# A Hymba block on one Trainium2 core: GLU's weights in plain blocks, 52 products ahead of u, and v's shifted rows on GpSimd's queue

## The chip, the core and the metric

One core of a Trainium2 chip runs the whole block as one program. The metric is the device time of one execution in microseconds (us), and kernels are compared by the median of their runs. A profile is of one execution.

## The reference

One layer: RMSNorm, one combined projection, a state space model (SSM) with a gated linear unit (GLU) beside stick-breaking attention, a shared output projection, and a gate from a per-layer embedding. 2048 tokens, 1024 channels, 8 heads of 64.

```python
h = x
hn = rmsnorm(h, mix_norm_g)
u, g_ssm, q, k, v, g_attn = split(hn @ w_in)            # 512 columns each
y_ssm = glu(gelu(s5(u)), w_glu, b_glu) * silu(g_ssm)      # val * sigmoid(gate) of z @ w_glu + b_glu
# attention in blocks of 128 queries, strictly causal
z = q @ k.T / 8
log_stay = where(strict, log_sigmoid(-z), 0)
later = cumsum(log_stay, reverse) - log_stay
weights = where(strict, exp(log_sigmoid(z) + later), 0)
y_att = (weights @ v) * silu(g_attn)
h = h + concat(y_ssm, y_att) @ w_out
h = h + sigmoid(rmsnorm(h) @ w_ple_gate) * (p @ w_ple_proj)
```

In stick-breaking attention the weight of a key is the difference of two neighbouring running products of 1 − sigmoid(z). So the kernel may multiply the running products by differences of neighbouring rows of v, and this is why it needs v beside v shifted by one row.

## The kernel before

**Tiles and number format.** The 2048 tokens are 16 tiles of 128 (NT), the 1024 channels 8 blocks of 128 (NC8). A float32 matrix is split into a high and a low part of type fp32r, and a product is three (high × high, high × low, low × high): `mm3` (L539, its three products are L544, L545, L546), `mm3x` (L714), and the three steps in `attn_proj` (L757) and `attn_block` (L824). A weight is loaded by `load_w`: DMA on SyncE's queue into a stage `wst` (L489), high part `w_w` on ScalarE (L494) and low part on VectorE (L79), or, where it has no scale, `split` (L516 and L68).

**Stages.** `phase_u` (0 to 142 us of the profile) makes u in 8 turns T of 256 tokens: 4 blocks of columns (ct) × 8 blocks of channels × 3 products. For T = 0 the loop over channel blocks is outside, so that a weight block is used as it arrives; ahead of its first product stand HOT = 18 products of a zero tile `idle` (L634) into the same bank, which the first real product overwrites. The norm of T = 2 and later is a chain: ScalarE squares and sums x (L601), VectorE and GpSimd make `rs_x` (L75, L510), ScalarE scales x (L603), TensorE turns it (`ps_x`, L529). Beside it VectorE computes the SSM's tables (`ssm_chain`). Then come the SSM with the gates and the first projections of attention (142 to 305), attention (305 to 1090), and the output projection with the embedding's gate (from 1090).

**Attention.** Four pairs of heads (hp 0 to 3) follow each other 8 steps apart in one loop over steps. In a step, `attn_block` works on one query tile of each active pair, and `attn_proj` makes q, k, v and the gate of the tile two steps ahead. The GLU, its weights (`glu_load`, two halves of four blocks `wst`, L489) and sums of weights run in the last ten steps and just before.

`attn_proj` leaves q, k, gate and v of a tile in `qn`. Then v − shifted v is formed on GpSimd:

```python
    nc.sync.dma_start(vb[1:], vr[:P - 1])
    if i + 1 < NT:
        nc.sync.dma_start(A.v[i + 1][:1].rearrange("p h d -> p (h d)"), vr[P - 1:])
    nc.gpsimd.tensor_tensor(vb, vr, vb, op=ALU.subtract)
```

The first transfer (L765) moves 127 rows of v down by one partition, the second (L767) the last row into the first row of the next tile; L768 subtracts when both have landed. Behind it on GpSimd stand the power for the norm of q and k (`rs_qk`, L510) and in `attn_block` the strict mask: `affine_select` (L831) on `px`, which ScalarE wrote (L828) and VectorE's scan (L833) reads. The scan releases the banks of `ps_z`; its result is turned (`ps_wt`, L529), made into `ws` (L847) and multiplied by v (`ps_o`, L855).

**Order.** The program's text doesn't set the order. `_ORDER` is a compressed table that lists, engine by engine, which of the remaining instructions comes next; `arrange` (L1387) turns neighbours in it into dependencies. The five engines are TensorE (PE), VectorE (DVE), ScalarE (ACT), GpSimd (POOL) and SyncE (SP), whose list holds nearly all DMA issues. Each engine works its list in order, so a waiting instruction holds what is behind it.

Of the kernel before, what the change touches and what calls it, by code (L numbers as in the profile page):

```python
# [723 lines left out]
def attn_proj(e, pool, A, i, xt=None):  # L724

    nc = e.nc
# [38 lines left out]
    nc.sync.dma_start(vb[1:], vr[:P - 1])  # L765
# [297 lines left out]
def hybrid_block_kernel(ctx: ExitStack, tc: tile.TileContext, x, xt, small, p, w_in, ssm_w_glu, w_out, w_ple_gate,  # L1063
# [237 lines left out]
    'xNFz^&Ye5w=XdQ|k#7)2EL&vhvP}?ZCaaM}WvJ^uX*cd)T)cPj$l_wgf@M&7KRa<E%Z?q}y_@+maldDoHqXi}Fph~u&_tD^CqxuE6p+t-=d&wB'
    '$Bq$6mmUWH^VQq#yYIe-vx^rm3iGo}h2HDLo+^lcXf<z*x?V?I%JY2w>3fApG)pu+y}Ek(^z`nNZ<v!Or>DPczHB}{RCWr{E3ZgH9T3qxj?&qb'
    '3H|MMyPLY`AYbp{7m>x$1vKC=?Q|Z5rAr6TG#a!eNeC{oM%y|Cu@|-5v_LH;?ssc)l3>NnX159A+SAkVRE%cAI_idDFYK0eAF#R|=E`=!Oq!eg'
    'x!eVNJ9hMXes{UMm4CJPBk}!d|H3K0*R`h|@tkJaQ>=a+p#!-ovomcs+xUBN5w@Jyn;}{zi5udOeUj+Ff`FE$rbIIw0JvAZUP5s@j$7zi7;cW^'
    '7{L$J>-G36%d~rOxv$&zv{u8W9>eO{^cLqA=I6I;nTG+eWbbEb4c%0Mo_z92{*pnu>^;JxZ!hFT=g(Jy!RO8WdI0-Ba_G=KPA$zl4iDrE=-Fpy'
    'o_SK}`plD0JmEY(jSE+p*d!<)VfK1Ig`U~13HDF-3)%b1WLe2a#?YZd?m-??)}Dl5q6YUXg62Y)eHhNE9TLpRFcprCk8Vnon4Fl!^B5@e0j_iX'
    '+3VM@KfUv*r$kMUJ$B>fwQEFIuksiwT|m&Don=q-W*&M7eI`0iM-fL&$FvKkQQ25Ha9~*YE5z`Jlp73enr^Sv`VhtW(Ff)8J<q;}u9H~G`>$TT'
    '`t;LRpL*(Q6PkSD%9U#bmwV(9t$tqo{vmPY4hM9TiY_$7X|Ta4+gy_TEYWMZh_4%Nq^0z+)*Ep4*6Zd|ubEG+h05aKBT(oIdI%L#9M8v_<3UH?'
    '#iXg@BomzgU%3*;>g+QJ;Cm$P^;`(M71Az<I~pS*hdrs@YQZ7Ui$>$c#w~iDKJ?Ou;umB30BAlE+r4@7rsqBNRNnA45G^;GOHGlBXf9VU{*HGF'
    '@s2`<O{^6*O4_R}$>(N-ZS+F|`K%bSjB63Paw{wN94?Wb**8KOT6T^Q*Om@9A6l2T2^}Ay0&x_{Qz;f241{FB`D%7JAfzt1d&4x$<LbJkAnDQw'  # L1310
# [10 lines left out]
    'wXk=J$~4B5t!NxJ)2sDul%vE(%G-}5I(B!vGFHy}8n=h<8)s?biu#xG9*4>{y56PMrSqKe5v!~{?ZLm9L0M0e8k4?f>PvM^tg2aUYg`7Y$7bu}'
    'u6K^d-aa<_o*gdLh@<1WUgj9LZnBY5=u~C-p&68_*8kSj7ui&@sXkX}56bH=cPhMUR_=ZMbEz`jzK!Ye?P^roBlN-No_l{ihSFzZuiHVHFVX*)'
    'yDMtX<(bNOj8;Wqx+khUlU5muUq38e`3EWAH-A4;dqDMGTkSt1+P4JP&eziL-M2pR3B=h~Ub%Iv+7rb(Fi^4iT2s|38(GG=QwY^Z%s*eEYK_sw'
    'C=CZAOH#7Kqxiwsh9ANfG;Z>%%Q)jgYyBf*eat?Z^s7+nnP;BoOr%e}^(iT1bEL$_AAcO5#jYcU3Y`k6+l^Zcd?!VrQ5oK>Z!&`b_udb`ca6ru'
    'zv2N}`OLA>gX2-yqUUdqp{lvB54F~VDo<W|0wC_O#~!<M>B^N+jH&Aw#~-ZsI^Dl84nvpA#?XT*QQe^Yl$WoSjlPOC7>5Ez=g*`b;g3!&9Xocf'
# [119 lines left out]
```

## Time and profile before

| | us |
|---|---|
| median of three runs | 1454.87 |
| lowest and highest | 1451.27, 1454.92 |
| profiled execution, its time | 1450.63 |
| its span | 1448.6 |
| attention's stage in it | 305 to 1090 |

In the rows of a profile, PE is TensorE, PEld its weight loads, DVE VectorE, ACT ScalarE, POOL GpSimd, SP or SPq SyncE, which issues DMAs. A timeline row gives start and length in us, engine, line, operation, written tile <- read tiles, shapes, and in brackets how long the engine stood idle ahead of it and what ended this. A row of the view of waits gives engine, tile and line that waited, what it waited for, the us in total, how often, and the longest. Lines are those of the kernel before; behind line 680 the changed kernel's numbers are one smaller.

### The profile page before, as it was taken

What the parts mean: (1) busy time and instruction counts of PE and PEld (TensorE: products, weight loads), DVE (VectorE), ACT (ScalarE), POOL (GpSimd) and SP (SyncE); (2) the same over time, 40 slices, a digit from 0 to 9 for tenths busy, and PEclk for the clock granted to TensorE, in tenths of its full rate; (3) what the DMA queues carried; (4) which work ended last, traced back from release to release, by engine and by line L of the source; (5) the groups of instructions that cost most, each with busy time, mean ns of one, the idle gap of its engine ahead of it and who ended that gap; (6) DMA issues with size and microseconds to landing.
All of it is one profiled execution on the core that took longest, in us unless ns stands there. A gap on an engine that the chain in (4) does not pass through costs nothing.

```text
span 1448.6 us, 33549 instructions
## 1 busy us (share of the span) xinstructions
PE 1426.0 (98%) x13062; PEld 1207.9 (83%) x13062; DVE 1024.3 (71%) x1832; ACT 809.4 (56%) x1763; POOL 473.8 (33%) x518
## 2 busy tenths in 40 slices
...
GB/s 321 290 305 207 238 127 176 234 148 174 140 128 107 149 109 128 132 117 133 117 103 129 123 163 168 243 228 193 146 210 263 174 163 204 179 80 95 102 66 66
DMA packets 179341, 238.21 MB, mean 164 GB/s; under 512 B 65792, under 2 KB 121328, under 8 KB 168048
## 3 DMA queue, kind: packets, MB, share of 16 engines
...
q14 instruction: 54, 0.44, 0.1%
...
## 4 chain that ended last, share of the span: by engine, by line
PE 88%; DVE 5%; ACT 2%; issue 2%; DMA 2%; POOL 1%; SPq 0%; ACTq 0%; DVEq 0%; POOLq 0%
PE ps_q L757 23%; PE ps_o L855 9%; PE ps_z L824 7%; PE ps_wt L529 5%; PE ps_g L719 4%; PE ps_g L721 3%; PE ps_g L720 3%; PE ps_h L719 3%; PE ps_h L721 3%; PE ps_h L720 3%; PE ps_sg L544 1%; PE ps_sg L545 1%; PE ps_u L544 1%; PE ps_sg L546 1%; PE ps_u L546 1%
## 5 line engine op out<-in xcount | busy, mean ns | idle before, releaser
L833 DVE TENSOR_TENSOR_SCAN px<-px,ps_z 128x512 f32<-128x512 f32 (+3 forms) x320 | 339.3, 1086 | 113.8 <-ACT px L828 66.4
L757 PE MATMUL ps_q<-w_w,xt 64*128 64x512 f32 x2784 | 366.1, 397 | 0.0
L757 PEld LDWEIGHTS ps_q<-w_w,xt 64*128 64x128 f32 x2784 | 259.4, 185 | 45.3 <-issue 1.2
L847 ACT ACTIVATE ws<-ps_wt 128x512 f32<-128x512 f32 (+3 forms) x320 | 155.3, 536 | 85.8 <-PE ps_wt L529 83.8
L828 ACT ACTIVATE px<-ps_z 128x512 f32<-128x512 f32 (+3 forms) x320 | 159.1, 538 | 76.5 <-PE ps_z L824 59.0
L855 PE MATMUL ps_o<-ws,v 128*64 128x128 f32 x2176 | 136.9, 276 | 0.5 <-DVE yat L68 0.5
L510 POOL TENSOR_TENSOR rs_qk<-rs_qk,mhalf 128x4 f32<-128x4 f32 x64 | 66.2, 1035 | 211.5 <-DVE rs_qk L75 207.5
L824 PE MATMUL ps_z<-k,q 64*128 64x512 f32 (+3 forms) x960 | 132.3, 373 | 1.7 <-DVE px L833 1.7
L855 PEld LDWEIGHTS ps_o<-ws,v 128*64 128x64 f32 x2176 | 117.1, 137 | 15.0 <-issue 10.1
L529 PEld LDWEIGHTS ps_wt<-ident,px 64*128 64x128 f32 x2176 | 88.3, 138 | 31.5 <-ACT ws L847 10.1
L529 PE MATMUL ps_wt<-ident,px 64*128 64x64 f32 x2176 | 98.8, 225 | 3.3 <-ACT ws L847 2.2
L824 PEld LDWEIGHTS ps_z<-k,q 64*128 64x128 f32 x960 | 87.1, 186 | 16.6 <-DVE px L833 2.9
L831 POOL TENSOR_SCALAR_AFFINE_SELECT px<-px 128x128 f32<-128x128 f32 x128 | 38.9, 313 | 179.6 <-ACT px L828 178.0
L516 ACT ACTIVATE yr<-sx 128x512 fp32r<-128x512 f32 x64 | 38.9, 626 | 80.3 <-PE ps_g L721 46.6
L544 PE MATMUL ps_u<-xt,w_w 128*128 128x256 f32 x256 | 67.1, 293 | 5.4 <-ACT w_w L494 5.4
L768 POOL TENSOR_TENSOR v<-qn,v 128x128 f32<-128x128 f32 x64 | 30.6, 479 | 118.9 <-DMA v<-qn 117.9
L1044 POOL TENSOR_TENSOR sg<-sg,h 128x512 f32<-128x512 f32 x28 | 41.4, 1481 | 84.5 <-DVE sg L68 74.6
L546 PE MATMUL ps_u<-xt,w_w 128*128 128x256 f32 x256 | 66.3, 290 | 0.0
L545 PE MATMUL ps_u<-xt,w_w 128*128 128x256 f32 x256 | 65.0, 288 | 0.0
L68 DVE TENSOR_TENSOR yr<-sx,yr 128x512 fp32r<-128x512 f32 x64 | 57.1, 914 | 6.1 <-ACT yr L516 5.1
L68 DVE TENSOR_TENSOR qn<-qn,rs_qk 128x256 f32<-128x256 f32 x64 | 30.6, 478 | 33.0 <-POOL rs_qk L510 32.9
L544 PE MATMUL ps_sg<-xg,w_w 128*128 128x256 f32 x192 | 53.1, 297 | 0.8 <-DVE sg L68 0.7
...
## 6 DMA issues: line engine op xcount, KB each, us to landing
...
h<-h SPq DMA_DIRECT2D x64, 256.0 KB
wst<-in_w_in_dram SPq DMA_DIRECT2D x48, 256.0 KB
...
out_dram<-sg SPq DMA_DIRECT2D x31, 256.0 KB
h<-in_x_dram SPq DMA_DIRECT2D x28, 256.0 KB
...
```

The costliest lines, as they stand in the source:

```text
L68: nc.vector.tensor_tensor(out, a, b, op=op)
L529: e.nc.tensor.transpose(ps[h][:, 64 * k:64 * k + 64], v[r], e.ident[r, r])
L544: mm(out, wh, xh, start=first, stop=False)
L546: mm(out, wl, xh, start=False, stop=last)
L719: mm(out, xh, wh, start=first, stop=False, skip_group_check=more)
L720: mm(out, xh, wl, start=False, stop=False, skip_group_check=more)
L757: nc.tensor.matmul(o, xt[r, a, c], A.w[c][r, b], start=c + s == 0, stop=c == NC8 - 1 and s == 2)
L824: nc.tensor.matmul(z[:, :n], q[half[h], a], A.k[ch][half[h], b, :n], start=s == 0, stop=s == 2)
L828: nc.scalar.activation(px[:, :n], z[:, :n], AF.Sigmoid, scale=-(HD ** -0.5))
L833: nc.vector.tensor_tensor_scan(rv, rv, z[:, :n][:, ::-1], initial=1.0 if carry[h] is None else carry[h], op0=ALU.mult, op1=ALU.bypass)
L847: nc.scalar.activation(dst, ps, AF.Copy, bias=1.0, scale=-1.0)
L855: nc.tensor.matmul(po[half[h], :P], A.v[sb][:, h], w[:, h, b], start=sb == i, stop=sb == 0)
```

## The change

1. HOT goes from 18 to 52.
2. `glu_load` takes plain blocks of 128 rows (`row_blocks`, L502). Before, a block was a view of four pieces of 32 rows each, since rows were ordered by group and channel; now `kernel()` orders the rows of `ssm_w_glu` on the host as it lays out the inputs.
3. The two transfers of `attn_proj` (L765, L767) are issued by GpSimd. GpSimd has 149 DMA issues where it had 25, SyncE 660 where it had 784. The copy from a `vl` tile (L739) stays with SyncE.
4. `_ORDER` is another table.

```diff
-HOT = 18
+HOT = 52
...
 def glu_load(e, k):
-    rows = e.w_glu[0].rearrange("(g h) n -> h g n", h=GH)
-    return load_w(e, [rows[4 * c:4 * c + 4, :, 512 * k:512 * k + 512] for c in range(4)], 512, None)
+    return load_w(e, row_blocks(e.w_glu[0], 4, 512 * k), 512, None)
...
-    nc.sync.dma_start(vb[1:], vr[:P - 1])
+    nc.gpsimd.dma_start(vb[1:], vr[:P - 1])
     if i + 1 < NT:
-        nc.sync.dma_start(A.v[i + 1][:1].rearrange("p h d -> p (h d)"), vr[P - 1:])
+        nc.gpsimd.dma_start(A.v[i + 1][:1].rearrange("p h d -> p (h d)"), vr[P - 1:])
     nc.gpsimd.tensor_tensor(vb, vr, vb, op=ALU.subtract)
...
 _ORDER = (
-    'c-q}uYpfmDRbG3~d*;kJa~}6?U!QxguYLWve#g$kkJye~KZ4`bj+3}foV006lQfMCrH$3JO_b6$luDpN140y)0u>b%s8B?ODt;h-R4pJ>sRAJt'
+    'c-pmGYm8mTUH{LV_v_wsU%Pj`ue)CFuGf#X_Yr&T*l}VzjvvV;an_GGiJf=zsvAsGS}UX>q)F5^NR&dO2niZR5P^t@1O-*7;sZjWN&z9HBE$#O'
...
+        if name == "ssm_w_glu":
+            a = _np.ascontiguousarray(a.reshape(-1, G, GH, 2 * G * GH).swapaxes(1, 2).reshape(a.shape))
```

What the new table does is read from the order of the instructions. A row is line, operation, written tile <- read tiles, and shape; a tile's number tells apart tiles of one name. In the changed kernel the number of a tile that is made behind the `idle` products is 34 higher (`v_10338` is `v_10372`).

On **GpSimd**, in the middle of attention (650 to 668 us of the profile before), where v of one tile and `px` of another meet. Before:

```order
L510 TENSOR_TENSOR rs_qk_10487<-rs_qk_10487,mhalf_146 128x4
L768 TENSOR_TENSOR v_10017<-qn_10422,v_10017 128x128
L510 TENSOR_TENSOR rs_qk_10818<-rs_qk_10818,mhalf_146 128x4
L768 TENSOR_TENSOR v_10338<-qn_10755,v_10338 128x128
L831 AFFINE_SELECT px_10680<-px_10680 128x128
L831 AFFINE_SELECT px_10686<-px_10686 128x128
L510 TENSOR_TENSOR rs_qk_10903<-rs_qk_10903,mhalf_146 128x4
L831 AFFINE_SELECT px_10950<-px_10950 128x128
```

After:

```order
L767 TENSOR_TENSOR v_10051<-qn_10456,v_10051 128x128
L764 DMA v_10372<-qn_10789 127x128
L510 TENSOR_TENSOR rs_qk_10852<-rs_qk_10852,mhalf_146 128x4
L767 TENSOR_TENSOR v_10372<-qn_10789,v_10372 128x128
L830 AFFINE_SELECT px_10714<-px_10714 128x128
L764 DMA v_10457<-qn_10872 127x128
L766 DMA v_10873<-qn_10872 1x16x8
L830 AFFINE_SELECT px_10720<-px_10720 128x128
L510 TENSOR_TENSOR rs_qk_10937<-rs_qk_10937,mhalf_146 128x4
```

The transfers now stand in GpSimd's list, each ahead of its subtraction (`v_10372` is formed two rows behind its issue), and the selects of `px_10714` and `px_10720` (before: `px_10680`, `px_10686`) still come behind that subtraction, now with the next tile's two issues around the first of them.

On **SyncE**, the same place, with the loads of GLU's weights (`wst` of `in_ssm_w_glu`). Before:

```order
L489 DMA wst_10937<-in_w_in_dram 128x4x128
L729 DMA xt_11201<-hn8_68 128x2048
L489 DMA wst_12824<-in_ssm_w_glu_dram 128x1x512
L765 DMA v_10338<-qn_10755 127x128
L489 DMA wst_12829<-in_ssm_w_glu_dram 128x1x512
L859 DMA ya12_110<-yat_10256 128x128
L729 DMA xt_11287<-hn0_60 128x2048
L767 DMA v_10839<-qn_10838 1x16x8
L765 DMA v_10423<-qn_10838 127x128
L859 DMA ya4_102<-yat_10332 128x128
```

After:

```order
L489 DMA wst_10971<-in_w_in_dram 128x4x128
L728 DMA xt_11235<-hn8_68 128x2048
L489 DMA wst_12858<-in_ssm_w_glu_dram 128x512
L489 DMA wst_12863<-in_ssm_w_glu_dram 128x512
L858 DMA ya12_110<-yat_10290 128x128
L728 DMA xt_11321<-hn0_60 128x2048
L858 DMA ya4_102<-yat_10366 128x128
L489 DMA wst_12868<-in_ssm_w_glu_dram 128x512
L489 DMA wst_12873<-in_ssm_w_glu_dram 128x512
```

The transfers of v are gone from between the loads of GLU's weights, and these read 128 rows of 512 columns instead of the view with four pieces.

On **VectorE**, during u (40 to 48 us of the profile before), where `rs_x` of a tile stands among the SSM's tables (`pwr`, `pwi`, `cm`, `pr`, `bbs`). Before:

```order
L68 TENSOR_TENSOR pr_fr_541<-pr_fr_541,pr_den_538 128x32
L68 TENSOR_TENSOR cm3_508<-pwi_490,pwr_489 128x64
L68 TENSOR_TENSOR pr_t2_540<-pr_nr_537,pr_li_344 128x32
L68 TENSOR_TENSOR cm1_506<-pwi_490 128x64
L68 TENSOR_TENSOR pwi_490<-cm2_507,cm3_508 128x64
L68 TENSOR_TENSOR pr_fis_542<-pr_t1_539,pr_t2_540 128x32
L68 TENSOR_TENSOR bbs_558<-bsw_351,pr_fr_541 128x512
L68 TENSOR_TENSOR pwr_489<-cm0_505,cm1_506 128x64
L75 TENSOR_SCALAR rs_x_1069<-ss_1067 128x1
```

After:

```order
L68 TENSOR_TENSOR pwr_489<-cm0_495,cm1_496 128x32
L68 TENSOR_TENSOR pr_t1_539<-pr_nr_537,pr_lr_343 128x32
L75 TENSOR_SCALAR rs_x_1103<-ss_1101 128x1
L68 TENSOR_TENSOR cm2_507<-pwr_489,pwi_490 128x64
L68 TENSOR_TENSOR cm1_506<-pwi_490 128x64
L68 TENSOR_TENSOR cm0_505<-pwr_489 128x64
L68 TENSOR_TENSOR cm3_508<-pwi_490,pwr_489 128x64
L68 TENSOR_TENSOR pwr_489<-cm0_505,cm1_506 128x64
L68 TENSOR_TENSOR pr_fr_541<-pr_t1_539,pr_t2_540 128x32
L68 TENSOR_TENSOR pwi_490<-cm2_507,cm3_508 128x64
L68 TENSOR_TENSOR pr_t2_540<-pr_nr_537,pr_li_344 128x32
```

`rs_x_1069` (after: `rs_x_1103`) stood behind the whole step of the power table and `bbs`; now it stands ahead of that step.

More of the change, by code (lines that the diff above doesn't have):

```diff
@@ L1301 @@
[L1301 to L1310, printed above, removed]
@@ L1321 @@
[L1321 to L1325, printed above, removed]
@@ new lines @@
+    '*tzrK&I=cIuJ7Er6PrI2uM+OLXLT+<aA0;eUY?1MAc!5SJ7U2&|K7C=zZF{>9tJRz?*{g$lmd%@xdz}RbUFtPAX%NIrKQf|;$r8{OLum0U*}lo'
+    '?Afz-EG*n3C^kPau`9vEL_9Y)K0Y%}=){wgWAW(NSlmyxhvFpU6Z+|o<Jov-Cf>2SiX_G>)62^Vk>le?;TZEna&W}0#l=<^#g;6bdCX0vB}Aai'
+    'NUsJ}I10!~fVH(Xm;&NKv4wl@osQ!v!pW(rnB?GSXZP;Ih)ySt4@^v~&^Wdc#^RBYIl7t_^bMw7C)(mTlioEP$+>gqK#f5A)Z0qZsrOa8{icH5'
+    'yLSVPzKPhref!&LWu@5!xPE<tz)j9R^;CoaR)gR&_|lV~O}E~|)T(m;x1YWpAPix05@2ckh(~H5_38xrQmOFmzTfoyG2h?j69QCT9=GRJJa7Yq'
+    '>${$ddLKouJ58oya+ECwpgF*)wWt*ZuFpL*=|WYpae*yU@9^x;RjV`A9XoVIN6{pbf?2*#1$Q(WC+y=n_BkRm*sfp^KMM;B{C$2NcGBM+y&O-B'
@@ new lines @@
+    'hU6xOp$6Lk+AwAC{ErgRCWJIb&r60lj+6u=3^9ZaLC!Sp!q0+R*;A3ri5(LYI7JgECKDZ+9hWFa6@w?9kdEL=GNy-!Mfcwiq?9BAa5q5_5|vXK'
+    'ZiAJTgDVGKHTp3{zs8L*KzeYXPdqX5_`{4VS4J*hHZENP)cc1JEF2Ru$Mw2Tvf)tMw-b!RaEPH-bKrp<7=UGSX^CuiYD^S_!aU>yYN+cHPkGX7'
+    'H6|ieYW&qeQ4Lb!h=3Ph<T+8tD_4+1moM+UL^J?gc=X!Eiva6*(}N&-c^1yzi)IUnJ#}j2#0j+S#{iDt7#d1RPux{%T1Y)+Nu_aOIvp2hKQ%k7'
+    'RX4j*@_bicK8K&j03LyBS7gBJPp_}9Kla#T`1{Iw<)McvmG$)pvC<mfa^{TV3_Ivu95g*$@l?bNLfSr!icO0n+5x}9<9t&ISE__MeqQ<N8;a6b'
+    'F+a?UF?z4-058128j2rOKo}qIk_vF=sZ%64#|d}db=O_Q7;d(TZtWo6GnUewDm%*06d59*3BdvLe9=v80>bc>D0~q)^ZfPe&riXNFMf^zT?$BY'
@@ new lines @@
+    '9|nC1=jp-)Qkki#bg(1I-(zA?1c&j?gXoEd?IF8IL(ybF8}+4~2icFzMrIx&FNKn`zYpTqclAN68{y<8Fw3|j2b}=bHV3wke%={&O>+)Q4AH+m'
+    'n?`RN>jNMLZfyW0njjR%^zs%_r1aSwgu{<B((=nW^oI-tme%7T<46uL0Qp`9;V|P0qj>+>97Ga&%a3db;dXw6d1(~GUF`9T8=_eI={`t|Q>?eX'
+    'A*4>ZByg0nt=QiCsyuCHd|TZ*tuXuoUdw?b|0YAEvB~J4W0Cwv2S9Z5B15$Cfj*>qno-@057e#GX~u7>@)Q>EO;w(n3Eos$l2IjAt^_ai;a*0+'
+    'Y>552nuFvQTl{OawNx%`f2^_u8$xC$&xibq@^zJ^-lf<LMqY+rV)R>^ud6IcPWc!F`BpNV${{YGShu(;78^52YqpxC&q10c65l(Lw^Vr&dh;CS'
+    'h<pIVtBK?kH8*cJ#IELZinT>T^Q*Tw-m27z#r{im>r|Yryktr%TeEVaHG}vs6#kmZQa>kO&7oK(($_nSW%wUep2Vj8rz%gyR(_(gB(pL|ri=I!'
@@ new lines @@
+    'Ri4DceXO!H$VcZbq-e-*sja1cubsD?`Bd&_#j|fr=ht<XL|@+2TT8_j|4Wspyo}1o^0RX*o0E@J%joz>Wl3U>&G@xqE8kLC5=qP3?TzGIYTt^A'
+    'B7RquCy~{SEo26vcaUrhN+Mmi8nNWccrI@Usd=6uHspK`o8d;@stih^ZSSb^RJ6oj&VeE>(F>8HK@pckOBeef{-G?gI-P?qK>A8I5sHygnOA+S'
+    '53-{9@&HIn5-s%FB8iBe-XbIhD01afb?YRt%4XxJ@2T=sDL^=w*N&ka$|Xr6DB(sw$7GzsF{$~|0OadrkUsuRWvO?im*Vf$ty59|L@U3q%2T_5'
+    'KTuhcJ3mxe>U7HXZ+qpfKStVWqE=q*gS1<W6w|(6*X2nh@c&eniW>bNsyr3z{j<uFSg+m~sL1z0(kPy)Jc1fzz4J+=caSBQv2JEX*&CM*wxRFq'
+    'EJ@$r)>}&=`5RfP{wD&2e^FW5tpAf8k9;(hPyIb_#;1!n9JE%Ic7C?#>j%0#6{-4IXG!GeBb}w9eS1%5N#ws+qs$`@ila7)ss2G_NvJE|o%;)w'
@@ new lines @@
+    'C9#!*v|}?#XvnWht~2tsYh#M@mbN%n@x&Wh)IsYek@LKDE#8?Qp;-8S>zV<!2$^eH8I)^_tS-fiogRR^9_2x~<<atI8Cl5~Zsb5wmdvm0Pz{Q*'
+    'E^dgQ=U&#v`&wJw%aV~uoVJx+EP+I55^-G}fX`+ZYqOD<=zCEg2YI*8G7{T39+T4YKJxZqGwElK)@0VUx<8ip_+qhp?;9jzgHr#l*TzxYM!Q}j'
+    'U9z?rY^(Cz6AJ!Sm8XrkDwgSoDoe$ku_9-sue|Tbr}C(5<A`fB>9dc@WK2KQy{Twx#A0sbGX{D3GOwSHfb&Vl@{cM@MXvvqDo<mK;+RCYg#y}r'
+    'Nj>IAw@CRIPawW<Bl=02Z{ECFG*1hRr=Nc2nP*A^D0xu!hTdA5$l<?LmPCwys<JdVKr4n_@?a>xXqNW#IaE)+{T-%H)!*XhN8M6!I1>ewZ<l3|'
+    'khZsuge}F<-nj898rrXX<;It96pQ2r6w#|!AAPJ`So6vu)dz(ew=$v<M95?3=lW2rEn84x5b_&Q{g6{(=>zaQ20cc|r`&0f4IdrLqxZb4F9uML'
@@ new lines @@
+    'zetcr;PS}y+O=z?4=|H+D)rCm0ZY9A34#V~6W&VFQsXA!&~v$mlVu8=f1Fi#$ow~|WE)+IZVo_E$_Is6vOwJ^Oj)~pd2Q|D+Jy^i>+9vg<q1Zq'
+    'pOn)KgCggA+Fa!DBtt~M|Cuk<5OFWY88YzowTIS7(AU-;SX--?;^<Kn;=`+llEY2KVi8AqF1@`6KTwG&RX^V(5pmjU%AH?MgTz+^H*WkQ;zn`9'
+    '^7{2BpM2>h=3$ZF*BF;Boj-pewFkv1C^}^cjXqTGVfui7OX&L^r(*4QFg$xleS?#@%ku5iJo>{?@n<xdB$5~C%Y!(Z_uqeinPkcc)1c_j@$+Z7'
+    'ln<Cb!IXY4>W;LMS&8rBhv<A?{murqq}WQC?rim;NV#9?uT}o2qO^wq((ufp4W*_bN72kMIi8jSA0LF=(JROuD@%^8T2-ik5gLZ!8Lmr5vP?P$'
+    '^}nX1?y=FIrl*Ym-OTl~O^?tTwgpXa>W&=K7SZE6Nnas;_xLI~mJD`{_MRg?&6*sg!vWw3cu0M|zfs8!6Vu^KTU(Z;O|yGkR8A;DmF^DkekKHx'
@@ new lines @@
+    'BaG>RGdkf`qcd)*dzO#S+kxM|%o~Z?Q55kGc`_a)D-StYoj<r{*O)9w1}JAI`B<(>&iXZ*;3h>vuOmA{k)7@cc1cc7I`YQ65h4MeoV~<uc$Bu*'
+    'cq4bu2Ogv3+#lE^D%hxLiuTeO&Jrj(UnpQX@?>OkUOG84JOXVx%{M#@zMN0?yf48kOaOcVwr|(^g|xNy6K&S^Y-1$b@{*;RoCk&;!A$4eOrKCu'
+    'l_=uF>)A<T$Js@50W&i*-P43HIy$;T8Z;mpt>aB0w?~MgyQ7nlmvF4x`4XQb#9Ej9i*)J~8?W-g%b?Q<Nb2b5vk`Tln91yFo@Ub|xnU(7mod=1'
+    'LUQUCx+k$gM$XRl=<zP+>3r|X$|HysSY8&|{RbX+Kn5YlEtzpz%XG=$6Y?Q{nlhN7IipjTnzW&<hfQL&2JP@&DCK5OahB-_^?um580=qwy?aSP'
+    '=g}Ud&wLt&F$#L5iqs_A(m48k`-EwBj|z^Cf=ldZRl%r7H6u0x!xxH8deOl1OqaKQlKQvZ22ATRFw^(?bhr=4ecxydBdm&i`rH?d6fW@_3zl!~'
@@ new lines @@
+    'vAAaumyYX(Za~Vheb^atTGeV{Pa>pvjR`sicO<V{96Xpwna`&z$L8k7X6+dyDzw0-fwHFPC@}z{;`T0UettfAZ-P%zkF%{Id&sh_1M#TTt|gY!'
+    'vJ{_`&V=FMBHRWm!7?oE-Mb(5@G0rh*;(7JwySUw;5gEJ3_rG<!$&r{iz&}@mMnC4(kXl&Rj}rhQLAxx5YUlS8aA0fON+V4`aXaYzP!9IKz|#M'
+    'O_(3AlZ|L|+pKYImQ|54&NSHe@Z6~ibZtrLL&87OYHI2&1z%GgdShZY>@wa{FfnJ1&$_>^MrTI1zpF;4zM-ZxjM(ilqly7)g{2z@3=T>v7#evE'
+    '6Xv)%X6_m_cWyH)Ge1#gG;M}c=8x5n75KG(QhppXp%MH@d7r9U(+hOX*HtfwJRP`bhQF^o+UEo7d&>G#6nl;A)annFNhc=^{d)@3hssbyDjlFl'
+    '4z(0CenV-+C#<Vcr0O`E{+F;KuEKAqUr;ZTz}aA1))%cWJZpX4v7fT6CoJol2<FwRB)0H~ei@rY<vo94&$DZA|9#lN8GzYSXb`Y*bpq8`q20hr'
```

86 lines of the change are left out of this document (31 added, 55 removed).

## The prediction

> **What bounds the kernel now.** I read the busy shares first, then the chain that ended last, then TensorE's own waits.
>
> ```profile
> span 1448.6 us, 33549 instructions
> PE 1426.0 (98%) x13062; PEld 1207.9 (83%) x13062; DVE 1024.3 (71%) x1832; ACT 809.4 (56%) x1763; POOL 473.8 (33%) x518
> ...
> PE 88%; DVE 5%; ACT 2%; issue 2%; DMA 2%; POOL 1%; SPq 0%; ACTq 0%; DVEq 0%; POOLq 0%
> ```
>
> TensorE works through 98% of the span and carries 88% of the last chain. An edit can win in two ways only: it removes one of TensorE's waits, which are 1448.6 − 1426.0 = 22.6 us together, or it makes products shorter. It can lose by a new wait. The view of TensorE's waits names the larger ones:
>
> ```profile
> PE ps_u L544 <- ACT w_w L494: 5.4, 1, 5.4
> PE ps_wt L529 <- ACT ws L847: 2.2, 6, 0.6
> PE ps_z L824 <- DVE px L833: 1.7, 2, 1.0
> PE ps_sg L544 <- DVE sg L68: 1.3, 2, 0.7
> PE ps_x L529 <- DVE xt L68: 1.2, 4, 0.4
> PE ps_wt L529 <- ACT g L803: 1.1, 2, 0.6
> ...
> PE ps_tq L529 <- ACT ws L847: 1.0, 1, 1.0
> ```
>
> The change meets the first row (52 products stand before that wait) and the third (GLU's loads and v's transfers, below). The others hang on ACT and DVE, whose work it doesn't cut.
>
> **Part 1: the 52 products.** TensorE's timeline at the start, and two stretches of equal length:
>
> ```profile
> 1.05 4.02 PE L634 MATMUL ps_u<-idle 128*128 128x256 bf16 x18 [1.05 <-DVE warm L1095]
> ...
> 10.43 0.80 PE L544 MATMUL ps_u<-xt,w_w 128*128 128x256 f32 x2 [5.36 <-ACT w_w L494]
> ...
> 16.11 0.41 PE L546 MATMUL ps_u<-xt,w_w 128*128 128x256 f32 x1
> ...
> 17.00 0.28 PE L545 MATMUL ps_u<-xt,w_w 128*128 128x256 f32 x1
> ```
>
> ```profile
> 10.43:16.42 5.99, 5.97 (x26) 1.00 1.04 392
> 16.42:22.41 5.99, 5.99 (x52) 1.00 0.80 248
> ```
>
> The columns are length, busy time of TensorE with its products, granted clock, DMA share and GB/s. The granted clock reads 1.00 in both, but the first stretch issues 26 products, 5.99/26 = 0.23 us each, and the second 52, 0.115 us each. One product lasts 0.41 us at 16.11 and 0.28 at 17.00: TensorE runs at half rate until about 16.4 us, 6 us after it begins to work without a pause. The 18 products of before end at 10.43 − 5.36 = 5.07 us, so each took (5.07 − 1.05)/18 = 0.223 us: half rate throughout. Then it stood still and began again at half rate.
>
> If 6 us of work are always needed, the step comes at 1.05 + 6.0 = 7.05 us after 6.0/0.223 = 27 products; the other 25 take 25 × 0.115 = 2.9 us and end at about 10.0 us, before the weights of 10.43 us. The real products then start at full rate. All 26 at full rate would save 26 × (0.23 − 0.115) = 3.0 us, but the weights come one block after the other:
>
> ```profile
> 9.65 0.72 ACT L494 ACTIVATE w_w<-wst,gmix 128x512 fp32r<-128x512 f32 x1 [1.07 <-DMA gmix<-in_small_dram]
> 12.64 0.72 ACT L494 ACTIVATE w_w<-wst,gmix 128x512 fp32r<-128x512 f32 x1 [1.15 <-DMA wst<-in_w_in_dram]
> 14.22 1.93 ACT L494 ACTIVATE w_w<-wst,gmix 128x512 fp32r<-128x512 f32 x3
> ```
>
> A faster TensorE waits for them: a block is 4 × 3 = 12 products, 1.4 us at full rate, and the first two blocks come 3.0 us apart. From 14.22 us three come within 1.93 us. By 16.3 us TensorE had done 21 real products (the 26 less five of ps_row); at full rate it can have done the 36 of the first three blocks, the third of which has its high half at 14.22 + 1.93/3 = 14.9 us. The lead is 15 × 0.12 = **1.8 us** (0 to 3.0).
>
> The Trainium skill, "TensorE: Matmul & The Clock Gate", Part 1, says that the full clock comes after about one busy window of some 3.4 us, that the window runs freely, and that one idle window takes it back. The trace agrees with the loss of the clock in a pause of 5.36 us; its 4.0 us without a step, and 6 us to one, fit a free window only. By that rule the step could come as early as 4.5 us, and the term stays 1.8.
>
> What could eat the lead is the next place where data set the pace, T = 2 and 3 of u:
>
> ```profile
> 45.60 2.75 POOL L510 TENSOR_TENSOR rs_x<-rs_x,mhalf 128x1 f32<-128x1 f32 x1 [10.66 <-DVE rs_x L75]
> ...
> 48.38 1.15 ACT L603 ACTIVATE x<-x,rs_x 128x1024 f32<-128x1024 f32 x1 [1.62 <-POOL rs_x L510]
> ...
> 49.58 0.65 PE L529 MATMUL ps_x<-ident,x 64*128 64x64 f32 x14 [0.92 <-ACT x L603]
> ```
>
> TensorE waits there for VectorE, then GpSimd, then ScalarE. The new order sets that rs_x eleven instructions earlier on VectorE, ahead of a 128x512 product among others, so I keep the 1.8 and count its loss as a rival.
>
> **Part 2: GLU's loads in plain blocks, and v's rows on GpSimd's queue.** These belong together; here is the third row of the waits, at 668 us:
>
> ```profile
> 656.44 0.65 SPq L765 DMA_DIRECT2D v<-qn  x1
> 657.20 5.56 SPq L489 DMA_DIRECT2D wst<-in_ssm_w_glu_dram  x1
> ...
> 666.46 0.45 POOL L768 TENSOR_TENSOR v<-qn,v 128x128 f32<-128x128 f32 x1 [5.75 <-DMA v<-qn]
> 666.88 0.53 POOL L831 TENSOR_SCALAR_AFFINE_SELECT px<-px 128x128 f32<-128x128 f32 x2
> ...
> 667.20 0.69 DVE L833 TENSOR_TENSOR_SCAN px<-px,ps_z 128x256 f32<-128x256 f32 x1 [1.61 <-POOL px L831]
> ...
> 667.94 0.50 PE L824 MATMUL ps_z<-k,q 64*128 64x512 f32 x2 [1.04 <-DVE px L833]
> ```
>
> v's rows are issued at 656.44 and land at 666.46, 10.0 us later, beside a GLU load that holds SyncE for 5.56 us. GpSimd works in order: its subtraction of v waits, and behind it stand the two selects, behind these VectorE's scan, behind that TensorE. The same chain stands at 694 us:
>
> ```profile
> 682.84 0.66 SPq L765 DMA_DIRECT2D v<-qn  x1
> 683.61 5.66 SPq L489 DMA_DIRECT2D wst<-in_ssm_w_glu_dram  x1
> ...
> 692.99 0.46 POOL L768 TENSOR_TENSOR v<-qn,v 128x128 f32<-128x128 f32 x1 [5.04 <-DMA v<-qn]
> ...
> 694.73 0.50 PE L824 MATMUL ps_z<-k,q 64*128 64x512 f32 x2 [0.62 <-DVE px L833]
> ```
>
> They cost 1.04 + 0.62 = **1.7 us**. In the new order no GLU load stands beside a transfer of v on one queue. The view of DMA issues (count, KB each, median us to landing) has a time only for GpSimd's queue:
>
> ```profile
> yq<-ys POOLq DMA_DIRECT2D x2, 256.0 KB, 5.6
> ...
> v<-qn SPq DMA_DIRECT2D x64, 63.5 KB
> ```
>
> 256 KB land in 5.6 us, and v's transfer is a quarter of that, so v should land some 6 us after its issue, at 663 instead of 666.5, and the selects run when ScalarE's px is there. I take all 1.7; the bounds are 0 (it lands no earlier) and 2.2, if 0.5 of other waits goes along.
>
> What GpSimd takes on: 16 tiles × 4 head pairs of v's rows, and of the last row one less in each pair, 64 + 60 = 124 issues. The nearest rows for the price of one:
>
> ```profile
> 5.09 0.57 POOL L208 DMA_DIRECT2D bst<-in_small_dram  x1
> ...
> 70.99 1.15 POOL L650 DMA_DIRECT2D u<-uq  x1 [0.42 <-ACT uq L647]
> ```
>
> 124 × 0.57 to 1.15 is 71 to 143 us; nearer the first row (small pieces), I take 0.7, 87 us. Between 305 and 1090 us GpSimd is busy for 200 us of 785 (busy time of PE, PEld, DVE, ACT and POOL in this order):
>
> ```profile
> 305.00:1090.00 785.00, 778.52 (x9017) 642.73 (x9017) 561.53 (x906) 483.55 (x1118) 200.28 (x309) 1.00 0.48 151
> ```
>
> With the issues it comes to about 37%, so its total hides them: 0. If that cover fails at single selects, it is the rival below. SyncE loses these issues; TensorE waits for none of its queue but in the two places above, so that is 0 too. Later reads of v by TensorE (ps_o) come 26 us of its work behind ps_q and cover any landing here.
>
> **Part 3: the order.** TensorE's own sequence hardly moves, and the thin places (ps_wt on ws, ps_z on px) stand as they stood. I count 0; bounds are −3.4, half of the five other rows above (2.2 + 1.3 + 1.2 + 1.1 + 1.0 = 6.8), and +3, as many new waits.
>
> **Sum.** −1.8 − 1.7 + 0 + 0 = −3.5. The profiled execution took 1450.63 us (span 1448.6 and 2.0 around it) and would come to 1447.1. The median of the three runs is 1454.87, 4.2 above that execution; I carry the difference over: 1454.87 − 3.5 = **1451.4 us**. What a measurement can tell from no change is 0.3%, 4.4 us: faster is below 1450.5, slower above 1459.2. The forecast lies just inside "same".
>
> **The rivals.**
> - **The order wins more.** Half of the 6.8 us goes as well: 1451.4 − 3.4 = 1448.0. For it: all those waits are under 1.1 us, and a little slack takes each away. Against: VectorE's and ScalarE's work is the same.
> - **The lead is lost** at 45 to 50 us, where x arrives when it arrives: 1454.87 − 1.7 = 1453.2. For it: the wait of 10.66 us on GpSimd for VectorE's rs_x.
> - **The clock doesn't come, or the 52 run over.** All at half rate, 52 × 0.223 = 11.6 us, end at 12.65 us, 2.2 after the weights. It decides at a step later than 8.1 us (32 slow products end at 8.2, 20 fast ones at 10.5). 1454.87 + 2.2 − 1.7 = 1455.4. For it: 4.0 us of such products didn't bring the step.
> - **GpSimd's queue turns into the bound (slower).** Each transfer of v is now issued by the engine that also makes the selects, and its subtraction still stands ahead of some. VectorE waits for selects already:
>
> ```profile
> DVE px L833 <- POOL px L831: 46.3, 46, 3.3
> ...
> POOL v L768 <- DMA v<-qn: 117.9, 45, 5.8
> ```
>
>   GpSimd waits for v 45 times, 2.6 us in the mean, and only twice does TensorE feel it, at (1.04 + 0.62)/2 = 0.83 us. If v lands later than 664.63 − 656.44 = 8.2 us (ScalarE's px is ready at 665.08, the subtraction takes 0.45), both stalls stay, and each of the other places that becomes thin costs 0.83. At 8 of them: 1454.87 − 1.8 + 6.6 = 1459.7; from 8 on it is slower. For it: 1.15 us for one issue beside a busy VectorE. Against: 5.6 us for four times the bytes. The Trainium skill, "SBUF — State Buffer", in its trap "DVE blocks DMA", says that GpSimd can't write descriptors while VectorE runs a two-port operation and names SyncE's or ScalarE's queue as the cure, which speaks against this edit; the longer issue would agree, and it is why I give this case more than a rest.
>
> **Chances.** The forecast 0.44, of which 0.15 falls below 1450.5 by its own spread of some 2 us; more won by the order 0.25 (faster); lead lost 0.10 and clock late 0.07 (same); GpSimd's queue 0.14, of which 0.12 slower and 0.02 same. Faster 0.15 + 0.25 = 0.40; slower 0.12; same 0.48. The range reaches from 1454.87 − 3.0 − 2.2 − 3.4 = 1446 and 1.5 of scatter, 1444.5, to 1458.5, the clock's case with the +3 of new waits (1455.4 + 3); beyond it lie most of the slower cases and the lowest of the faster.
>
> **What would show it.** Right: products of L634 at 0.115 us from about 7 us on, the wait at the first real product under 1 us, L545 at 0.28 from the start with waits for w_w between, no ps_z wait at 668 and 694, v landing in 6 us. Wrong: real products of 0.41 after 10.43; ps_z waits on px in more than 8 places; GpSimd's issues above 1.2 us; or waits for ws and sg that double, which would be the order.

## The result, and the profile after

| | before | after |
|---|---|---|
| median of 20 runs each, us | 1454.55 | 1457.28 |
| lowest and highest, us | 1451.27, 1457.52 | 1452.75, 1462.43 |
| profiled execution, its time and span, us | 1450.63, 1448.6 | 1461.8, 1459.8 |
| a second profile of after, its span, us | | 1455.9 |

The ratio is 1.0024, with a 95% interval of 1.0015 to 1.0032: 3.5 us slower (the two medians are 2.7 us apart), where 3.5 us faster was forecast. It is within the 0.3% and within the range, but the sign is wrong. The page of the changed kernel:

```profile
span 1459.8 us, 33618 instructions
PE 1433.6 (98%) x13096; PEld 1217.7 (83%) x13096; DVE 1027.1 (70%) x1832; ACT 806.7 (55%) x1763; POOL 539.4 (37%) x642
...
PE 86%; DVE 5%; DMA 3%; issue 2%; ACT 2%; POOL 2%; POOLq 0%; DVEq 0%; ACTq 0%; SPq 0%
```

TensorE is still the bound. It is busy 7.6 us longer (1433.6 against 1426.0), with only 34 products more, and it waits 3.6 us longer (26.2 against 22.6). GpSimd took on 65.6 us (539.4 − 473.8), 0.53 us for each of 124 issues, below my 0.7.

This profile shows one of the slowest executions. Each run lists the mean granted clock, and the changed kernel's 20 times go with it: 1452.75 and 1453.97 us at 0.999, 1457.37 to 1462.43 us at 0.992 and 0.993. This is the spread and not the loss: on one chip the mean granted clock of 12 runs of the change was 0.9956, and that of 29 runs of before 0.9951. So single profiles can't be subtracted; I tell apart what every profile of a program shows from what changes from one to the next.

**The start.** TensorE's timeline and four windows (length, busy, granted clock, DMA share, GB/s) of this profile:

```profile
1.05 7.66 PE L634 MATMUL ps_u<-idle 128*128 128x256 bf16 x52 [1.05 <-DVE idle L632]
9.55 0.61 PE L544 MATMUL ps_u<-xt,w_w 128*128 128x256 f32 x3 [0.84 <-ACT w_w L494]
10.01 0.28 PE L545 MATMUL ps_u<-xt,w_w 128*128 128x256 f32 x1
...
12.17 1.01 PE L546 MATMUL ps_u<-xt,w_w 128*128 128x256 f32 x3 [1.41 <-DVE w_w L79]
...
13.83 0.41 PE L545 MATMUL ps_u<-xt,w_w 128*128 128x256 f32 x1
```

```profile
10.00:12.00 2.00, 0.76 (x7) 0.91 1.03 397
12.00:14.00 2.00, 1.83 (x8) 0.50 1.05 394
...
20.00:22.00 2.00, 2.00 (x12) 0.53 0.01 2
22.00:24.00 2.00, 2.00 (x19) 1.00 0.32 49
```

The 52 products ended at 8.71 us, inside the time without weights, and the first real products ran at 0.28, as forecast. TensorE ran out of weights twice, for 0.84 us ahead of them and 1.41 us behind the first eight, and from 11.6 to 21.9 us the granted clock was 0.5. The step to full rate that I wanted earlier came, was lost, and came back at 21.9 us, where before had it from 16.4 us.

**v on GpSimd.** Groups of v's tile (durations in ns: lowest, median, highest) and the view of DMA issues (last column: median us to landing):

```profile
L764 POOL DMA_DIRECT2D v<-qn x64: 539/586/639, 192.9 to 1024.1; - x64
...
v<-qn POOLq DMA_DIRECT2D x64, 63.5 KB, 3.7
```

An issue never takes over 0.64 us and lands after 3.7 us in the median, where one on SyncE's queue beside GLU's loads took 10.0. TensorE's waits for px at 668 and 694 us are gone from this profile and from every other one with GLU's plain blocks. The trap of "SBUF — State Buffer" in the Trainium skill, that descriptors of GpSimd's queue starve beside VectorE, does not show in these rows.

**New waits.** TensorE's waits in the second profile:

```profile
PE ps_pack L355 <- ACT lt L352: 1.5, 1, 1.5
PE ps_u L546 <- DVE w_w L79: 1.5, 1, 1.5
PE ps_b L404 <- ACT stB L344: 1.2, 1, 1.2
PE ps_h L718 <- ACT yr L516: 1.2, 2, 0.6
...
PE ps_u L544 <- ACT uq L647: 1.0, 1, 1.0
PE ps_h L720 <- DVE yr L68: 0.9, 1, 0.9
```

Against before, ps_pack, ps_u's low half and uq are new, ps_h waits 2.1 us instead of 0.3, and ps_b 1.2 us for stB instead of 0.5. Which edit brings which is what the runs had to tell.

### The profile page after: what moved, and what is told of

The parts are those of the page before. It is cut to its first block, busy times and chain, and to the rows that moved or that the text cites. A ratio compares the mean times of both kernels' runs of the same rounds, so it can differ in the third digit from the quotient of the medians.

```text
span 1459.8 us, 33618 instructions
## 1 busy us (share of the span) xinstructions
PE 1433.6 (98%) x13096; PEld 1217.7 (83%) x13096; DVE 1027.1 (70%) x1832; ACT 806.7 (55%) x1763; POOL 539.4 (37%) x642
## 4 chain that ended last, share of the span: by engine, by line
PE 86%; DVE 5%; DMA 3%; issue 2%; ACT 2%; POOL 2%; POOLq 0%; DVEq 0%; ACTq 0%; SPq 0%
PE ps_q L756 24%; PE ps_o L854 8%; PE ps_z L823 7%; PE ps_wt L529 5%; PE ps_g L718 3%; PE ps_g L720 3%; PE ps_g L719 3%; PE ps_h L720 3%; PE ps_h L718 3%; PE ps_h L719 3%; PE ps_sg L544 1%; PE ps_sg L546 1%; PE ps_sg L545 1%; PE ps_u L546 1%; PE ps_u L544 1%
## 5 line engine op out<-in xcount | busy, mean ns | idle before, releaser
L764 POOL DMA_DIRECT2D v<-qn x64 | 37.4, 584 | 147.7 <-DVE qn L68 65.1
L544 PE MATMUL ps_u<-xt,w_w 128*128 128x256 f32 x256 | 66.9, 296 | 3.0 <-ACT uq L647 2.2
L546 PE MATMUL ps_u<-xt,w_w 128*128 128x256 f32 x256 | 68.3, 297 | 1.4 <-DVE w_w L79 1.4
L545 PE MATMUL ps_u<-xt,w_w 128*128 128x256 f32 x256 | 67.0, 294 | 0.4 <-DVE xt L68 0.4
L68 DVE TENSOR_TENSOR qn<-ps_q,part 128x512 f32<-128x512 f32 x48 | 32.9, 686 | 34.8 <-ACT part L762 31.3
L766 POOL DMA_DIRECT2D v<-qn x56 | 29.8, 533 | 74.3 <-DVE qn L68 40.8
```

Of the source, the lines that this page charges most:

```text
L68: nc.vector.tensor_tensor(out, a, b, op=op)
L544: mm(out, wh, xh, start=first, stop=False)
L546: mm(out, wl, xh, start=False, stop=last)
```

## The experiments

Ratios are to the kernel before on the same chip, each with its 95% interval. Three second profiles at the end, of one execution each, are not in the table.

| kernel | ratio | interval |
|---|---|---|
| before, 52 products | 1.0005 | 0.9994 to 1.0015 |
| before, GLU plain | 0.9977 | 0.9966 to 0.9989 |
| before, v on GpSimd | 1.0018 | 1.0007 to 1.0028 |
| all three, old order | 1.0005 | 0.9990 to 1.0020 |
| all three, new order (the change) | 1.0025 | 1.0011 to 1.0038 |
| the change, old order from 1083 us on | 1.0008 | 0.9996 to 1.0019 |
| the change, 18 products | 1.0037 | 1.0025 to 1.0049 |
| the change, v on SyncE | 1.0054 | 1.0041 to 1.0066 |
| the change, one pair on GpSimd exchanged | 1.0026 | 1.0013 to 1.0040 |
| before, new order on PE, DVE, ACT | 1.0060 | 1.0046 to 1.0075 |
| GLU plain, clock held | 0.9975 | 0.9963 to 0.9987 |

**First set: one edit back, or one edit alone.** My theory after the first profile was the clock (C): the 52 win the clock early and lose it again. The rivals were GpSimd's queue (G) and the order (O).

```diff
-HOT = 52
+HOT = 18
```

> The changed kernel with 18 products ahead of u again, everything else (loads, v on GpSimd, new order) kept. Theory C (clock): the 52 bring the full clock early, TensorE then runs out of weights, and the pauses of 0.84 and 1.41 us take the clock back until 21.9 us; without the 34 the granted clock reads 1.00 from 0 to 36 us and the median falls by 2 to 5 us, to 1452 to 1455. Theory G (GpSimd's queue): the time stays near 1457. Theory O (the new order has more waits): stays near 1457 too.

```diff
-HOT = 18
+HOT = 52
```

> The kernel before with 52 products ahead of u and nothing else. Theory C: the granted clock falls to 0.5 for about 10 us at 12 to 22 us in most executions, and the median is 2 to 4 us above before. Theories G and O: the time is that of before, or the 1.8 us less that I forecast.

Theory C fell as the account of the loss: 1.0037 without the 34 products, no faster than with them, and 1.0005 with them alone. What it said of the clock holds. In the kernel before with 52 products the clock falls at 12.7 us, after pauses of 0.68 us ahead of the first weights and 0.53 us ahead of their low half:

```profile
12.00:14.00 2.00, 1.63 (x10) 0.66 1.05 402
14.00:16.00 2.00, 2.00 (x10) 0.50 1.05 387
...
20.00:22.00 2.00, 2.00 (x19) 1.00 0.09 18
```

But the 18 products are no safer: three profiles with 18 have the clock at 0.5 around 10 to 20 us too (GLU plain, v on GpSimd, and the new order on three engines). The start is a matter of the execution either way.

```diff
-    nc.gpsimd.dma_start(vb[1:], vr[:P - 1])
+    nc.sync.dma_start(vb[1:], vr[:P - 1])
...
-        nc.gpsimd.dma_start(A.v[i + 1][:1].rearrange("p h d -> p (h d)"), vr[P - 1:])
+        nc.sync.dma_start(A.v[i + 1][:1].rearrange("p h d -> p (h d)"), vr[P - 1:])
```

> The changed kernel with v's transfers back on SyncE's queue, at the places that they have in the kernel before; 52 products, plain GLU loads and the rest of the order kept. Theory G: 2 to 3 us faster than the changed kernel, about 1454.5. Theories C and O: as the changed kernel, 1457 within 1.

The reverse edit in the kernel before:

> The kernel before with v's transfers on GpSimd's queue and nothing else (18 products, GLU's view, own order). Theory G: 2 to 4 us slower than before. Theories C and O: as before, or up to 1.7 us faster where the stalls at 668 and 694 us go.

Theory G has it half: on GpSimd's queue v costs 1.0018 in the old order, but in the new one it is worth having; back on SyncE the ratio is 1.0054. In that profile TensorE waits 1.41 us at 696.5 us for a transfer of `xt`, which SyncE issues, and 0.91 us at 938.1 us for px, waits that the change's profiles don't have.

What GpSimd's queue costs in the old order can be seen in the kernel's traces. GpSimd at 626 us and VectorE behind it, with v on GpSimd (second profile), and then in before:

```profile
626.46 0.61 POOL L765 DMA_DIRECT2D v<-qn  x1
627.07 0.51 POOL L767 DMA_DIRECT2D v<-qn  x1
627.60 1.05 POOL L510 TENSOR_TENSOR rs_qk<-rs_qk,mhalf 128x4 f32<-128x4 f32 x1
...
628.68 0.43 DVE L68 TENSOR_TENSOR qn<-qn,rs_qk 128x256 f32<-128x256 f32 x1 [1.71 <-POOL rs_qk L510]
```

```profile
624.70 1.01 POOL L510 TENSOR_TENSOR rs_qk<-rs_qk,mhalf 128x4 f32<-128x4 f32 x1
...
625.74 0.43 DVE L68 TENSOR_TENSOR qn<-qn,rs_qk 128x256 f32<-128x256 f32 x1 [0.55 <-POOL rs_qk L510]
```

The two issues, 1.12 us, stand ahead of the norm's power (`rs_qk`). VectorE waits 1.71 instead of 0.55 us for it, its next scan of px ends at 630.29 us, and the product of ps_z that waits for this scan starts at 630.35, so that TensorE is 0.5 us later from there on. At 734 us two issues stand ahead of a pair of selects in the same way (they start at 735.58 instead of 735.11 us), and TensorE is another 0.5 us later at 742 us. Both profiles of this kernel show both places. In the new order, too, two issues stand between the selects of `px_10714` and `px_10720`, ahead of the second.

**Second set: what each part is worth.** GLU's plain blocks alone, with `glu_load` and the rows on the host as in the change:

> The kernel before with GLU's weights in plain blocks (rows ordered on the host) and nothing else. My forecast's part 2: SyncE is no longer held 5.6 us at 657 and 683 us, v lands earlier, ps_z's waits at 668 and 694 us shrink: 0 to 1.7 us faster than before. Rival: v's transfer lands 10 us after its issue whatever stands behind it, and the time and both waits stay.

The ratio is 0.9977, 3.3 us faster (1.6 to 4.9), where I had put 1.7 us. The cause was right. At the place of the first stall, GpSimd's and SyncE's timelines of this kernel:

```profile
666.75 0.46 POOL L767 TENSOR_TENSOR v<-qn,v 128x128 f32<-128x128 f32 x1 [3.10 <-DMA v<-qn]
668.09 0.29 POOL L830 TENSOR_SCALAR_AFFINE_SELECT px<-px 128x128 f32<-128x128 f32 x1 [0.89 <-ACT px L827]
```

```profile
659.37 0.64 SPq L764 DMA_DIRECT2D v<-qn  x1
660.11 2.93 SPq L489 DMA_DIRECT2D wst<-in_ssm_w_glu_dram  x1
```

v lands 7.4 us after its issue instead of 10.0, the load behind it holds SyncE 2.9 us instead of 5.6, and the select now waits for ScalarE and not behind v. Where I set the starts of the same instructions in both profiles of this kernel beside those of before, it gains 2.5 us between 650 and 710 us in both, so this belongs to the program.

The order alone, without the lists of GpSimd and SyncE:

> The kernel before with the changed kernel's order on TensorE, VectorE and ScalarE; 18 products, GLU's view, v on SyncE, and the orders of GpSimd and SyncE as before. Theory O (the order loses): 3 to 6 us slower than before. Theory G (GpSimd's queue loses): within 1.5 us of before. If the order was made for v on GpSimd's queue, it may lose here and not there; the next run tells.

And everything but the order:

> Everything of the change but the order: 52 products, plain GLU blocks, v on GpSimd's queue (issued where the new order has them), in the order before. Theory O: about before, or 1 to 2 us faster than it. Theory G: 2 to 3 us slower than before, as with v on GpSimd alone.

The order alone has 1.0060, everything but the order 1.0005. The three edits together give nothing in the old order (0.9977, 1.0018 and 1.0005 multiply to 1.0000), and the new order adds 0.0020, 2.9 us: the intervals overlap a little, but the medians of the two kernels' 12 runs on this chip, 1454.19 and 1457.40 us, are 3.2 us apart. That the order alone loses more, 8.7 us, fits the 1.0054 of v on SyncE. It isn't the price of the order by itself, though, since this kernel joins the lists of two tables. The change once more gave the 1.0025 of the table and the second profile:

> The changed kernel once more, on the chip of this set, for a second profile. If the granted clock's falls (12 to 22, 94 and 333 us in the first profile) and the 3 us scan of VectorE at 245 us are chance of the execution, some are missing or stand elsewhere; if they belong to the program, they are there again. Time 1.001 to 1.004 of before.

The two profiles agree within 0.1 us over long stretches and differ in a few jumps. The granted clock falls at 12 to 19 and 330 to 333 us in the second; the fall at 94 us is missing.

**Third set: where the order loses.** From about 1083 us on the lists of the order before stand on all engines, in front of that those of the change (only `_ORDER` differs).

> The changed kernel with the order before on all engines from about 1083 us on (output phase), the new order ahead of that. If the new order's loss sits in its four waits of the output phase (0.89, 0.58, 0.60, 0.70 us at 1097, 1124, 1142 and 1246 us, 2.8 us, against 0.25 in the order before), these go and the ratio to before falls from 1.0025 to about 1.0007 (2 to 3 us). Rival: the loss sits ahead of it (u, 946 us, or the granted clock), and the ratio stays above 1.002.

The ratio is 1.0008 against the change's 1.0025, taken on another chip: 2.5 us, as expected (the intervals overlap a little; the next kernel below, which keeps the new order, has 1.0026 on this chip). The second profile of the change shows the four waits, and the last row is the one larger wait of before in that phase:

```profile
1096.98 0.50 PE L720 MATMUL ps_h<-w_w,yr 128*128 128x512 f32 x1 [0.89 <-DVE yr L68]
...
1124.38 0.50 PE L718 MATMUL ps_h<-w_w,yr 128*128 128x512 f32 x1 [0.58 <-ACT yr L516]
...
1141.59 0.50 PE L718 MATMUL ps_h<-w_w,yr 128*128 128x512 f32 x1 [0.60 <-ACT yr L516]
...
1245.71 0.50 PE L718 MATMUL ps_g<-w_w,yr 128*128 128x512 f32 x1 [0.70 <-ACT yr L516]
```

```profile
1092.19 0.50 PE L721 MATMUL ps_h<-w_w,yr 128*128 128x512 f32 x1 [0.27 <-DVE yr L68]
```

With the old order at the end the first of the four stays at 0.94 us and the other three, 1.9 us together, go. So the new order hands TensorE the split operands of the output phase (`yr`, made by ScalarE and VectorE) too late. It shows in every profile: from the start of attention's last product (`ps_o`, L855) to the end of the span it is 368.5 to 369.3 us in nine profiles with the old order, 370.7 to 371.7 in six with the new one, and 369.9 in this kernel, 1.8 less than in the second profile of the change. The waits ahead of that phase (uq, stB, and the low half of the first weight) stay, and are no part of the 2.5.

The new wait for lt at 245 us has another cause. VectorE's scan and GpSimd's product beside it, in before, and then in the second profile of the change:

```profile
236.67 1.23 DVE L447 TENSOR_TENSOR_SCAN rot<-decf,rot 128x512 f32<-128x512 f32 x1
...
236.66 3.07 POOL L335 TENSOR_TENSOR stC<-pwr,cts 128x1024 f32<-128x1024 f32 x1 [6.92 <-DVE rot L68]
```

```profile
238.58 3.11 DVE L447 TENSOR_TENSOR_SCAN rot<-decf,rot 128x512 f32<-128x512 f32 x1
...
238.55 2.05 POOL L335 TENSOR_TENSOR stC<-pwr,cts 128x1024 f32<-128x1024 f32 x1 [6.89 <-DVE rot L68]
...
245.24 0.44 PE L355 MATMUL ps_pack<-ident,lt 128*128 128x128 f32 x2 [1.55 <-ACT lt L352]
```

One VectorE instruction releases both within 0.03 us. Either the scan takes 1.23 and the product 3.07, or the product 2.05 and the scan 3.11. In the second case TensorE waits 1.5 to 2.0 us for lt. I exchanged GpSimd's product with the one behind it (of the fourth SSM batch):

```diff
-L335 stC<-pwr,cts
 L450 swp<-swp,tabs
+L335 stC<-pwr,cts
```

> The changed kernel with one pair of GpSimd's instructions exchanged: the product stC<-pwr,cts (L335 before) of the fourth SSM batch behind the product swp<-swp,tabs (L450) that followed it. If VectorE's scan of rot (3.11 us at 238 us instead of 1.23) is held up by that product, which starts 20 to 30 ns ahead of it, the scan takes 1.2 us, TensorE's wait for lt (1.5 us at 245) goes, and the time falls by 1 to 2 us. Rival: the scan is long for another reason, or stC comes too late now and TensorE waits for it: no gain.

The scan is short and the wait for lt gone, as the theory said, but the ratio is 1.0026, as the rival said: the product starts 4.9 us later, at 243.42 us, and TensorE waits further on, 0.84 us for bn at 253.6 us and 1.26 us for sg at 265.7 us, where the change's profiles have no wait. How the one leads to the other was not traced.

Is a held clock worth anything? GLU plain with 60 products ahead of u, and more of them where TensorE would pause, at places that the order sets (10 ahead of block 0's low halves, 4 ahead of block 1, 5 ahead of the dg product):

```diff
-HOT = 18
+HOT = 60
...
+            fill = e.bank("ps_fill", "o")[:, :256]
+            for _ in range(19):
+                nc.tensor.matmul(fill, idle[:, :P], idle, start=True, stop=True)
```

> The kernel before with GLU's plain blocks, 60 products ahead of u, and 19 more of the same kind into a bank of their own in the pauses of u's first two weight blocks (10 ahead of the low halves of block 0, 4 ahead of block 1, 5 ahead of the dg product). Theory C: the granted clock stays 1.00 from its first rise on, u's real products run at 0.12 us each from the start, and the kernel is 1 to 3 us faster than GLU's plain blocks alone (ratio to before 0.9977), 0.9957 to 0.997. Rival: TensorE is limited by the weights there, and the clock's loss costs nothing that the data don't: 0.9977 or above.

```profile
10.00:12.00 2.00, 1.34 (x12) 1.00 1.03 390
12.00:14.00 2.00, 2.00 (x19) 1.00 1.06 402
14.00:16.00 2.00, 1.91 (x17) 1.00 1.05 387
16.00:18.00 2.00, 2.00 (x19) 1.00 1.05 382
```

The clock holds at the start, and the mean granted clock of 12 runs is 0.998, where GLU plain has 0.996. The time doesn't fall by an amount that can be told: 0.9975 against 0.9977. TensorE runs at full rate into weights that come as they come (the DMA share is 1.03 to 1.06 there).

**Last, second profiles.** Three kernels were profiled once more, to tell what belongs to a program.

> The kernel before with v's transfers on GpSimd's queue once more, for a second profile. If VectorE's scan of rot at 239 us is long (3.1 us) whenever v is on GpSimd's queue in the order before, it is long again, and 2.2 us of that edit's loss is this. If it is chance of the execution, it may be 1.23 us, and the profile is then about 2 us shorter at 250 us.

The scan is 1.23 us here, where it was 3.11 in this kernel's first profile.

> GLU's plain blocks alone once more, for a second profile. The waits of ps_z at 668 and 694 us stay away (they belong to the program); the granted clock's falls at 8 to 20 and 324 to 334 us may be elsewhere, shorter or missing (they belong to the execution); the scan is 1.23 or 3.1 us, by chance.

No fall of the clock at the start nor at 324 us now, but one at 242 to 245 us, no wait for ps_z, and the scan 3.12 us instead of 1.23.

> GLU's plain blocks with the products in the pauses once more. No fall of the granted clock ahead of 60 us, as in the first profile; TensorE at 100 us is 1.5 to 2.5 us ahead of GLU's plain blocks alone unless those had a start without a fall. The scan is 1.23 or 3.1 us, by chance: if 1.23, this is the shortest profile of all, about 1446 us.

The scan is 1.23 instead of 3.12 us, no fall of the clock ahead of the end, and a span of 1444.5 us, the shortest of all. At 100 us, though, TensorE is no further than in the second profile of GLU's plain blocks, within 0.1 us. That one ran at half rate until 16.7 us and had no fall between there and 100 us, the case that the expectation excepts: against such a start the 79 products win nothing here, though their first weights also came 0.5 us later (10.41 against 9.88 us).

Over 15 profiles with GpSimd's order in that batch as it was, the scan was long in 7, and three kernels showed it both ways. The kernel with the old order at the end shares its first 1083 us with the change and had it short. It is chance of the execution, and no edit's price.

**The versions that beat both kernels** are GLU's plain blocks alone, 0.9977, and the same with the clock held, 0.9975; the two can't be told apart.

## Why the prediction was wrong, point by point

- **What bounds the kernel**: right. The loss came as waits of TensorE. The lower rate of the profiled execution is no part of it, since the mean granted clock over the runs is that of before.
- **Part 1, −1.8 us: the term was 0** (1.0005, −0.9 to +2.2 us). The 52 end ahead of the weights, as worked out, and sooner: 7.66 us are some 16 products at 0.223 us and 36 at 0.115, so the step to full rate came at about 4.6 us and not at 7.05. The step that failed is "at full rate it can have done the 36 of the first three blocks": I counted high halves and let the low halves be there, and TensorE waits for the first low half, 0.53 us in the kernel before with 52 products and 1.41 us in the profile after. (The 21 products beside the 36 are 20, since four and not five were of `ps_row`; this moves the lead by 0.1.) I also took the full rate as kept once it was there. All seven profiles with 52 products have the clock at 0.5 for 3.4 to 10.2 us between 11 and 22 us, and the two with products in the pauses don't: the pauses take it back. Holding it brought nothing that can be told: the weights set the pace, and the stretch at 45 to 57 us levels what is left (v on GpSimd, second profile, was 2.4 us behind before at 40 us and 0.9 at 60). The rival "the lead is lost" was the nearer one.
- **Part 2, GLU's blocks: right in mechanism, −3.3 instead of −1.7 us.** Both stalls go. The interval, 1.6 to 4.9, holds the 1.7 too, but in the traces they are worth 2.5, more than my bound of 2.2: the view of waits (1.04 and 0.62) counts from the end of a product, which lasts 0.47 us, while the next one starts some 0.23 us behind it when nothing waits.
- **Part 2, v on GpSimd at 0: wrong, +2.6 us alone** (1.0 to 4.1). The step that failed is "its total hides them: 0". GpSimd has the idle time, and v lands early, but an issue delays what stands right behind it in GpSimd's list: at 626 us `rs_qk` by 1.1 us, at 735 us two selects by 0.5. I had also missed that GLU's plain blocks win the same two stalls without it. Against before, both profiles of that kernel win them back (2.3 us between 640 and 710 us) and give 2.0 us away in small steps: 0.6 at 220, 0.5 at 630, 0.5 at 740, 0.3 at 960 and 0.2 us at 1130. Only the one at 630 was followed link by link to the issues. The rest of the 2.6 stays open. A part may be a wait for ps_tq at 325 us, 1.16 us instead of 0.97: behind it the granted clock falls for 3.4 or 6.8 us in all ten profiles with v on GpSimd's queue or the new order, and in two of the six others. That this small difference decides it is not shown.
- **The slower rival** named GpSimd's queue with another mechanism: v landing after 8.2 us in 8 places. v landed after 3.7 us, and no ps_z wait came back in the view. It named the right engine, and that issues stand with the selects; its condition, v landing late, was wrong.
- **Part 3, the order at 0: the step that turned the sign.** It costs 2.9 us (1.0025 against 1.0005), inside my bound of +3, and some 2 of these are in the output phase. I had compared the orders where attention is thin, and said "TensorE's own sequence hardly moves". In the output phase it moves: in the 75 us behind attention before runs 26 products with `w_w` in one go (at 1140.4 us), the change never more than 16. The waits are for `yr` of ScalarE and VectorE, whose lists moved too; which list makes them isn't separated, since all went back together.
- **Sum**: 0.7 for the 52, −3.3 for GLU, +2.6 for v and +2.9 for the order come to +2.9 us, with 3.5 measured; each term is uncertain by 1.5 us or more either way.
